# A neighbourhood-attention stage that scores only the keys it needs

## The chip, the cores and the metric

The kernel runs on one core of one Trainium2 chip. The metric is the time of the device in microseconds (us); smaller is better. A core has TensorE (PE in the profile, with PEld for its weight loads), VectorE (DVE), ScalarE (ACT), GpSimd (POOL) and SyncE (SP), which work through queues of their own and wait for one another by semaphores. Transfers are issued by SP and ACT and carried by 16 DMA engines.

## The reference

One encoder block on 1024 tokens of 1024 features: RMS norm, one input projection, a convolution group and an attention group side by side, an output projection with a residual, then a SwiGLU feed-forward layer with a residual. The part that matters here is the attention. The tokens form a grid of 16 rows and 64 columns. Each query attends to a window of 8 rows and 16 columns that is clamped inside the grid, with a learned bias for the offset:

```python
col_start = jnp.clip(cols - kw // 2, 0, GRID_W - kw)      # kw = 16, GRID_W = 64
def row_block(r):
    row_start = jnp.clip(r - kh // 2, 0, rows - kh)       # kh = 8, rows = 16
    ...
    s = jnp.einsum("bqhd,brqchd->bhqrc", q_r, k_win) * scale
    s = s + bias
    p = jax.nn.softmax(s, axis=(-2, -1))
    return jnp.einsum("bhqrc,brqchd->bqhd", p, v_win)
```

There are 8 heads of 64 features. Everything is float32.

## The kernel before

The order of all instructions is written out by hand; each engine takes its own in that order. First come the projections for keys, for the convolution, for queries and for values, with the taps of the convolution on VectorE beside them. In the same time the tables of the bias are made in DRAM (`bias_tables`): `t1` is filled with a large negative number and gets the runs of `rpb`, `tf` is filled likewise and gets windows of `t1`. These small transfers are strung between the weight loads on SP's queue, six for each step (`behind`).

**Tiles of the attention.** The queries are cut into 8 tiles of 128: two halves of the grid's rows (`rh` 0 and 1, 8 rows each) by four blocks of 16 columns (`cb`). A tile `s_` takes its half and block from `order`, which goes through `cb` 0, 3, 1, 2 and both halves of each. A tile's scores are taken against a rectangle of keys, `AR` rows by `ncol` columns from column `c0` on (`WIN`). A step `i` is one tile and one pair of heads (`hp`); there are 32.

**One step.** `score_mm` (L680) multiplies the queries by the rectangle of keys into PSUM, 288 or 384 columns for each of the two heads. `score_max` (L693, VectorE) adds the table of the bias, which is the large negative number outside a query's window, and takes the maximum; `score_exp` (L698, ScalarE) the exponential and the sum; `score_norm` (L709, GpSimd) the scaling by the sum. `flip` (L720, TensorE) transposes the weights in three groups of four rows of keys, and `flip_out` copies them back to SBUF (L727 on VectorE, L729 on ScalarE). `weigh` (L739, TensorE) multiplies them by the values, group by group, and sums in PSUM. From step 4 on one round of the loop holds the scores of steps i and i + 1, the transposes of i - 3 and i - 2, and the weighing of i - 5 and i - 4. The next round's scores take the PSUM that the copy of L727 frees.

**Values.** `value_out` (L447) stores the values of each 128 tokens to `vd` in DRAM on ACT's queue. `load_vw` (L660) fetches from there, on SP's queue, one row of the grid at a time, the `ncol` tokens of a window: `ncol` rows of 512 numbers (2 KB), for one or two groups at once. `vw[cb, g]` is the group of grid rows 4g to 4g + 3 of window `cb`. `load_window` fetches all four groups. The tables are fetched by `table` (L647), also on SP's queue. The order on that queue around the stage is: tables of the first three tiles, values of window 0, values of window 3, tables, and from step 8 on the last table and windows 1 and 2, then weights of the output projection (`wo00`, `wo02`).

Of the kernel before, what the change touches and what calls it, by code (L numbers as in the profile page):

```python
# [6 lines left out]
F32 = mybir.dt.float32  # L7
# [5 lines left out]
P = 128  # L13
# [4 lines left out]
NH = 8  # L18
HD = 64
# [3 lines left out]
EPS = 1e-6  # L23
NEG = -1e30
GW = 64
AR = 12
SIDE = (16, 17, 18, 19, 20, 21, 22)
WIN = ((0, 24, 8), (8, 32, 0), (24, 32, 0), (40, 24, 0))


def layout(v):
# [33 lines left out]
def body(tc, a):  # L65
    from contextlib import ExitStack
    with ExitStack() as ctx:
        build(ctx, tc, a)


def build(ctx, tc, a):
    nc = tc.nc
    pe, act, dve, pool = nc.tensor, nc.scalar, nc.vector, nc.gpsimd
# [3 lines left out]
    dr = ctx.enter_context(tc.tile_pool(name="dr", bufs=1, space=bass.MemoryType.DRAM))  # L77

    def T(tag, shape, bufs, name, dt=F32):
        return sb.tile(shape, dt, tag=tag, bufs=bufs, name=name)  # L80

    def G(name, dt=F32):
        return T("G", [P, 1024], 21, name, dt)
# [4 lines left out]
    def H(name, dt=F32):  # L88
        return T("H", [P, 4096], 7, name, dt)
# [4 lines left out]
    def SM(name, n=8):  # L94
        return T("sm", [P, 8], 12, name)[:, :n]

    def mm(name):
        return ps.tile([P, 512], F32, tag="mm", bufs=4, name=name)

    def tp(name):  # L100
        return ps.tile([P, 512], F32, tag="tp", bufs=2, name=name)

    def cv(name):
        return ps.tile([P, 1024], F32, tag="cv", bufs=1, name=name)
# [14 lines left out]
    def lr(w):  # L119
        return w[:, :512], w[:, 512:]  # L120
# [127 lines left out]
    ident = T("ident", [P, P], 1, "ident")  # L248
# [24 lines left out]
    for _ in range(9):  # L273
# [1 line left out]
    pool.affine_select(ident, ones, pattern=[[-1, P]], compare_op=OP.is_equal, fill=0.0,  # L275
                       base=0, channel_multiplier=1)
    qgs = T("qgs", [P, 1], 1, "qgs")
    t1 = [dr.tile([NH, 16, 15, ncol], F32, name=f"t1{ty}") for ty, ncol in enumerate((24, 32, 24))]
    tf = {(rh, ty): dr.tile([16, 8, NH, AR * t1[ty].shape[-1]], F32, name=f"tf{rh}{ty}")
          for rh in range(2) for ty in range(3)}  # L280

    def rstd_of(ss, scale, name):
# [159 lines left out]
    vd = dr.tile([S, 512], F32, name="vd")  # L442
# [61 lines left out]
    def bias_tables():  # L504
        neg = G("neg")
        pool.memset(neg, NEG)

        def fill1(ty):
            n = 15 * t1[ty].shape[-1]
            nc.sync.dma_start(t1[ty].rearrange("h j u b -> (h j) (u b)"), neg[:, :n])  # L510

        def fill2(rh, ty):
            n = 3 * AR * t1[ty].shape[-1] if ty != 1 else 2 * AR * 32
            for o in range(0, NH * AR * t1[ty].shape[-1], n):
                w = min(n, NH * AR * t1[ty].shape[-1] - o)
                nc.sync.dma_start(tf[rh, ty].rearrange("j i h c -> (j i) (h c)")[:, o:o + w], neg[:, :w])

        def run(ty, j):
            b0, shift = ((max(j - 8, 0), 15), (j, 7), (min(j, 8), 7))[ty]
            o = b0 - j + shift  # L520
            nc.sync.dma_start(t1[ty][:, j, :, b0:b0 + 16], a["rpb"][:, :, o:o + 16])

        def rows_of(rh, ty, i):
            ncol = t1[ty].shape[-1]
            a0 = max(i - 4, 0) if rh == 0 else min(i, 4)
            u0 = a0 - i + (7 if rh == 0 else 3)
            nc.sync.dma_start(tf[rh, ty][:, i, :, a0 * ncol:(a0 + 8) * ncol],
                              t1[ty][:, :, u0:u0 + 8, :].rearrange("h j u b -> j h (u b)"))
        for ty in (0, 2, 1):
            fill1(ty)  # L530
        for ty in (0, 2, 1):
            aside_dma.extend(lambda ty=ty, j=j: run(ty, j) for j in range(16))
            for rh in range(2):
                aside_dma.append(lambda rh=rh, ty=ty: fill2(rh, ty))
        for ty in (0, 2, 1):
            for rh in range(2):
                aside_dma.extend(lambda rh=rh, ty=ty, i=i: rows_of(rh, ty, i) for i in range(8))
# [30 lines left out]
    for kp in range(4):  # L568
        parts = []
# [66 lines left out]


    def table(rh, ty):
        n = AR * t1[ty].shape[-1]
        src = tf[rh, ty].rearrange("j i h c -> (j i) (h c)")  # L640
        if rh == 0 and ty == 0:
            parts = [(G(f"tab{k}")[:, :n * min(3, NH - 3 * k)], 3 * k) for k in range(3)]
        else:
            parts = [(H(f"tab{rh}{ty}")[:, :NH * n], 0)]
        heads = []
        for w, h0 in parts:
            nc.sync.dma_start(w, src[:, h0 * n:h0 * n + w.shape[-1]])  # L647
            heads += [w[:, o:o + n] for o in range(0, w.shape[-1], n)]
        return heads


    vwt, vw = {}, {}

    def load_vw(cb, *gs):
        c0, ncol, _ = WIN[cb]
        if gs[0] % 2 == 0:
            vwt[cb, gs[0] // 2] = G(f"vw{cb}{gs[0]}").rearrange("p (g d) -> p g d", d=512)
        w = vwt[cb, gs[0] // 2]
        for r in range(4):
            nc.sync.dma_start(w[r * ncol:(r + 1) * ncol, gs[0] % 2:gs[-1] % 2 + 1, :],  # L660
                              vd.rearrange("(g r c) d -> r c g d", r=4, c=GW)[r, c0:c0 + ncol, gs[0]:gs[-1] + 1, :])
        for g in gs:
            vw[cb, g] = w[:4 * ncol, g % 2, :]


    k4 = kT.rearrange("p c (r w) -> p c r w", w=GW)
    order = [(rh, cb) for cb in (0, 3, 1, 2) for rh in range(2)]
    tab, et, es, pTs, os_, sums, pp, mx, cvs = {}, {}, {}, {}, {}, {}, {}, {}, {}
    at = []

    def score_mm(i):
        s_, hp = divmod(i, 4)
        rh, cb = order[s_]
        t = rh * 4 + cb
        c0, ncol, _ = WIN[cb]
        s2 = cv(f"s{i}") if i > 0 and i % 2 == 0 else None
        out = []
        for hh in range(2):
            s = (mm(f"s{i}{hh}") if s2 is None else lr(s2)[hh])[:, :AR * ncol]
            pe.matmul(s, qT[hh * HD:(hh + 1) * HD, hp, t * P:(t + 1) * P],  # L680
                      k4[hh * HD:(hh + 1) * HD, hp, rh * 4:rh * 4 + AR, c0:c0 + ncol], start=True, stop=True)
            out.append(s)
        return out

    def score_max(i, hh, s):
        s_, hp = divmod(i, 4)
        rh, cb = order[s_]
        if i not in es:
            et[i] = G(f"e{i}").rearrange("p (h n) -> p h n", h=2)
            es[i] = et[i][:, :, :AR * WIN[cb][1]]  # L690
            sums[i] = SM(f"rs{i}", 2)
        mx[i, hh] = SM(f"mx{i}{hh}", 1)
        dve.tensor_tensor_reduce(out=es[i][:, hh], in0=s[hh], in1=tab[rh, cb][2 * hp + hh], scale=-1.0,  # L693
                                 scalar=3.0e38, op0=OP.add, op1=OP.min, accum_out=mx[i, hh])
# [15 lines left out]


    def flip(i):
        s_, hp = divmod(i, 4)
        m = 4 * WIN[order[s_][1]][1]
        if i % 2 == 0:
            cvs[i] = cv(f"p{i}")
        pp[i] = lr(cvs[i]) if i % 2 == 0 else [mm(f"p{i}{hh}") for hh in range(2)]
        for hh, pt in enumerate(pp[i]):
            for g in range(3):
                pe.transpose(pt[:m, g * P:(g + 1) * P], es[i][:, hh, g * m:(g + 1) * m], ident)  # L720

    def flip_out(i, hh=None):
        m = 4 * WIN[order[i // 4][1]][1]
        w = et[i][:m, :, :384]
        pTs[i] = [w[:, h].rearrange("p (n q) -> p n q", q=P) for h in range(2)]
        if hh is None:
            dve.tensor_copy(w, cvs[i].rearrange("p (h n) -> p h n", h=2)[:m, :, :384])  # L727
        else:
            act.copy(w[:, hh], pp[i][hh][:m, :384])  # L729

    def weigh(i):
        s_, hp = divmod(i, 4)
        rh, cb = order[s_]
        if hp == 0:
            os_[s_] = tp(f"o{s_}").rearrange("p (c q) -> p c q", c=4)
        for g in range(3):
            for hh in range(2):
                c = (2 * hp + hh) * HD
                pe.matmul(os_[s_][hh * HD:(hh + 1) * HD, hp], vw[cb, rh + g][:, c:c + HD], pTs[i][hh][:, g],  # L739
                          start=g == 0, stop=g == 2)  # L740

    def half(name):
        w = H(name, F32R).rearrange("p (w k s) -> p w k s", w=2, s=512)
# [15 lines left out]
    def value(t):  # L759
        z = nat(2, t, mm if t < 6 else tp)  # L760
        step(lambda n_taps: (value_out(t, z), pump(n_taps)))
# [3 lines left out]
    def load_window(cb):  # L765
        load_vw(cb, 0, 1)
        load_vw(cb, 2, 3)
# [12 lines left out]
    both(0, s0)  # L780
    pump(200)
    value(6)
    load_vw(0, 0, 1)
    load_vw(0, 2)
    s1, s3 = score_mm(1), score_mm(3)
    step()
    score_norm(0)
# [92 lines left out]
    for i in range(4, 32, 2):  # L880
# [24 lines left out]
        if i > 4:  # L905
            weigh(i - 5)
# [541 lines left out]
    def quarter(w, o, t):  # L1448
        return w[:, o + t * 512:o + t * 512 + 512]
# [32 lines left out]
    for s, p in enumerate(SEQ):  # L1482
        for k in range(QF - 2):
            n = s * QF + k
# [23 lines left out]
    for half in range(2):  # L1508
# [4 lines left out]
        w = quarter(om["u"], 0, 3)[:, part_]  # L1513
# [17 lines left out]
```

## Time and profile before

| what | value |
|---|---|
| median of 3 runs | 1035.13 us (1034.98 to 1036.01) |
| the profiled execution | 1035.18 us, its span 1033.5 us |
| TensorE busy | 1024.3 us (99%) |
| VectorE, ScalarE, GpSimd busy | 782.3 us (76%), 478.7 us (46%), 436.0 us (42%) |
| transfers | 152.53 MB in 75084 packets, 42.5% of the 16 engines' span on SP's queue (q1), 0.9% on ACT's (q10) |
| attention stage | about 220 to 306 us after the span's start |

The profile is of one execution. Times in it are counted from the first instruction; the 1.7 us between the span and the profiled execution lie outside. A line like `L739 PE MATMUL o<-e,vw` names the line of the kernel, the engine, the operation and the tiles written and read. A busy TensorE is not one at its peak, since matmuls overlap. The chain that ended last is followed back from the last instruction: at each step to what released it.

### The profile page before, as it was taken

Reading aid. Unit: us, or ns where it says so; the run is one execution under the profiler, and the core shown is the slowest. Engines: PE = TensorE matmul, PEld = TensorE weight load, DVE = VectorE, ACT = ScalarE, POOL = GpSimd, SP = SyncE. Lnnn points to the kernel's source line nnn. Section 1 sums busy time; section 2 is a strip of 40 time slices with the busy share of each in tenths; the row PEclk is TensorE's granted clock in tenths of the full one; section 3 lists DMA queues with packets and bytes.
Section 4 is the critical chain, followed back from the end, with each engine's and each line's share of the span. In section 5 each row is a group of like instructions: output and inputs, shape, how many; then the busy total and the mean of one; then the engine's idle time right before and its main releaser. Section 6 shows DMA issues by size and latency. Waiting matters only on the chain.

```text
span 1033.5 us, 15158 instructions
## 1 busy us (share of the span) xinstructions
PE 1024.3 (99%) x5334; PEld 853.8 (83%) x5334; DVE 782.3 (76%) x1234; ACT 478.7 (46%) x1045; POOL 436.0 (42%) x345
## 2 busy tenths in 40 slices
PE   9999999999999999999999999999999999999998
PEld 7888888877787788877888888888888888888887
DVE  5788997896755376998787787787787767758874
ACT  7565348836866345523334334343342443433432
POOL 1036764524641345047776667567566200003210
PEclk9999999999999999999999999999999999999999
DMA  9426781337403621122434424434441696633631
GB/s 347 165 79 201 225 255 53 122 115 234 124 22 122 235 92 41 47 107 89 156 119 157 139 96 153 153 101 145 144 143 71 222 365 238 224 102 123 214 122 42
DMA packets 75084, 152.53 MB, mean 148 GB/s; under 512 B 13824, under 2 KB 22784, under 8 KB 74368
## 3 DMA queue, kind: packets, MB, share of 16 engines
q1 hardware_dynamic: 72992, 148.21, 42.5%
q10 hardware_dynamic: 2016, 3.36, 0.9%
q8 instruction: 42, 0.69, 0.3%
q14 instruction: 34, 0.28, 0.1%
HBM read 112.38 MB, written 44.76 MB: 152 GB/s over the span
## 4 chain that ended last, share of the span: by engine, by line
PE 93%; DVE 5%; ACT 1%; issue 1%; DMA 0%; ACTq 0%; DVEq 0%
PE B L115 5%; PE B L116 5%; PE B L117 5%; PE z L115 4%; PE z L117 4%; PE z L116 4%; PE D L115 3%; PE D L116 3%; PE D L117 3%; PE gl L117 3%; PE gl L116 3%; PE gl L115 3%; PE pj L115 3%; PE pj L116 3%; PE pj L117 3%; PE p L720 2%
## 5 line engine op out<-in xcount | busy, mean ns | idle before, releaser
L363 DVE SCALAR_TENSOR_TENSOR cv<-u,par,cv 128x1009 f32<-128x1009 f32 (+14 forms) x92 | 117.4, 1277 | 2.3
L389 POOL TENSOR_TENSOR pa<-pa,pr 128x1022 f32<-128x1022 f32 (+5 forms) x24 | 58.0, 2417 | 48.7 <-ACT pr L388 36.1
L107 ACT CAST op<-sr 128x512 fp32r<-128x512 f32 x77 | 47.7, 619 | 57.7 <-PE B2d L117 26.7
L1474 POOL TENSOR_TENSOR ou<-ou,resm 128x512 f32<-128x512 f32 x8 | 12.0, 1506 | 139.8 <-DVE ou L1465 126.1
L111 DVE TENSOR_TENSOR op<-sr,op 128x512 fp32r<-128x512 f32 x77 | 57.6, 748 | 16.5 <-ACT op L107 16.4
L709 POOL TENSOR_SCALAR e<-e,rs 128x288 f32<-128x288 f32 (+1 forms) x64 | 33.9, 545 | 41.8 <-DVE rs L707 40.1
L1024 DVE TENSOR_TENSOR ts<-gu,ts 128x512 f32<-128x512 f32 x40 | 46.3, 1158 | 0.7
L107 ACT CAST op<-wd 128x512 fp32r<-128x512 f32 x54 | 33.4, 619 | 28.5 <-DVE wd L1370 18.0
L698 ACT ACTIVATE e<-e,mx 128x288 f32<-128x288 f32 (+1 forms) x64 | 36.5, 572 | 18.8 <-DVE mx L693 16.9
L111 DVE TENSOR_TENSOR op<-wd,op 128x512 fp32r<-128x512 f32 x54 | 39.8, 738 | 1.7 <-ACT op L107 0.6
L693 DVE CUSTOM_DVE_ANT_0 e<-s,tab 128x288 f32<-128x288 f32 (+1 forms) x64 | 28.7, 503 | 13.6 <-PE s L680 13.6
L980 POOL TENSOR_TENSOR sq<-sq,sq 128x512 f32<-128x512 f32 x12 | 17.1, 1423 | 51.6 <-ACT sq L976 51.4
L1283 DVE TENSOR_TENSOR g<-D,g 128x512 f32<-128x512 f32 x22 | 15.2, 690 | 23.4 <-PE D L117 23.4
L416 ACT ACTIVATE sq<-z,r 128x64 f32<-128x64 f32 x96 | 28.3, 329 | 5.2 <-PE z L117 5.2
L1260 ACT ACTIVATE D<-D 128x512 f32<-128x512 f32 x22 | 12.8, 582 | 32.6 <-DVE D L1259 32.6
L388 ACT ACTIVATE pr<-u,par 128x1022 f32<-128x1022 f32 (+5 forms) x24 | 27.0, 1138 | 1.6 <-ACT vs L446 1.2
L720 PEld LDWEIGHTS p<-ident,e 128*96 128x96 f32 (+1 forms) x192 | 20.5, 133 | 6.8 <-POOL e L709 6.3
L115 PE MATMUL B2d<-op 128*128 128x512 f32 x66 | 25.8, 391 | 0.0
L117 PE MATMUL B2d<-op 128*128 128x512 f32 x66 | 25.7, 389 | 0.0
L116 PE MATMUL B2d<-op 128*128 128x512 f32 x66 | 25.7, 389 | 0.0
L739 PE MATMUL o<-e,vw 96*64 96x128 f32 (+1 forms) x384 | 24.7, 277 | 0.0
L720 PE MATMUL p<-ident,e 128*96 128x128 f32 (+1 forms) x192 | 24.4, 276 | 0.0
(1454 smaller groups left out, 3734.5 us busy)
## 6 DMA issues: line engine op xcount, KB each, us to landing
gu<-in_gu SPq DMA_DIRECT2D x44, 512.0 KB
sr<-sd SPq DMA_DIRECT2D x77, 256.0 KB
sd<-sd SPq DMA_DIRECT2D x22, 512.0 KB
wd<-in_wd SPq DMA_DIRECT2D x36, 256.0 KB
sd<-g SPq DMA_DIRECT2D x33, 256.0 KB
x<-in_x SPq DMA_DIRECT2D x8, 512.0 KB
xT<-in_xp SPq DMA_DIRECT2D x8, 512.0 KB
xd<-xT SPq DMA_DIRECT2D x16, 256.0 KB
```

The source lines that it names most:

```text
L107: act.copy(hi, src)
L111: eng.tensor_tensor(*[w[..., sl] for w in (lo, src, hi.bitcast(F32))], OP.subtract)
L115: pe.matmul(acc, lh, rh, start=start, stop=False, skip_group_check=True)
L116: pe.matmul(acc, lh, rl, start=False, stop=False, skip_group_check=True)
L117: pe.matmul(acc, ll, rh, start=False, stop=stop, skip_group_check=True)
L363: dve.scalar_tensor_tensor(acc[:, o], uc[:, i], dwk[:, c, t:t + 1], acc[:, o], OP.mult, OP.add)
L389: pool.tensor_tensor(pa[:, o], pa[:, o], pr[:, o], OP.add)
L693: dve.tensor_tensor_reduce(out=es[i][:, hh], in0=s[hh], in1=tab[rh, cb][2 * hp + hh], scale=-1.0, scalar=3.0e38, op0=OP.add, op1=OP.min, a ...
L698: act.activation(e, e, AF.Exp, bias=mx.pop((i, hh)), scale=-1.0, accum_out=sums[i][:, hh:hh + 1])
L709: pool.tensor_scalar(es[i][:, hh], es[i][:, hh], rs[:, hh:hh + 1], 1.0, op0=OP.mult, op1=OP.mult)
L720: pe.transpose(pt[:m, g * P:(g + 1) * P], es[i][:, hh, g * m:(g + 1) * m], ident)
L1024: dve.tensor_tensor(o, l, r, OP.subtract)
```

## The change

The rectangle of keys shrinks to what the reference allows: 11 rows for the upper half of the grid and 12 for the lower, and 23, 31, 31 and 24 columns for the four blocks (before: 12 rows, 24, 32, 32 and 24 columns). The scores, the tables of the bias, the exponential and the scaling get narrower with it. The values of windows 0, 1 and 2 are loaded 23, 31 and 31 rows at a time. The keys of the first tile (11 x 23 = 253) form two groups of 128 instead of three (four rows of keys each), so its values come in a layout of their own (`load_first`: twelve loads, the sixth row of the grid cut at the group's edge into 13 and 10), and the loads of groups 1, 2 and 3 of window 0, for the second tile, follow. Where the last group is not full (tiles with 11 rows), GpSimd writes zeros behind the scores before the transposes. The table of the first tile comes in two parts of four heads instead of three of three.

```diff
-AR = 12
-WIN = ((0, 24, 8), (8, 32, 0), (24, 32, 0), (40, 24, 0))
+AR = (11, 12)
+WIN = ((0, 23), (8, 31), (24, 31), (40, 24))
+NCOL = (23, 31, 24)
...
 def load_vw(cb, *gs):
-    c0, ncol, _ = WIN[cb]
-    if gs[0] % 2 == 0:
+    c0, ncol = WIN[cb]
+    if (cb, gs[0] // 2) not in vwt:
         vwt[cb, gs[0] // 2] = G(f"vw{cb}{gs[0]}").rearrange("p (g d) -> p g d", d=512)
...
+def load_first():
+    c0, ncol = WIN[0]
+    w = vwt["first"] = G("vwf").rearrange("p (g d) -> p g d", d=512)
+    for r in range(AR[0]):
+        for g in range(2):
+            a0, a1 = max(r * ncol, g * P), min((r + 1) * ncol, g * P + P)
+            if a0 < a1:
+                t = r * GW + c0 + a0 - r * ncol
+                nc.sync.dma_start(w[a0 - g * P:a1 - g * P, g, :], vd[t:t + a1 - a0, :])
...
+def width(s_):
+    rh, cb = order[s_]
+    return AR[rh] * WIN[cb][1]
+
+def groups(s_):
+    n, m = width(s_), P if s_ == 0 else 4 * WIN[order[s_][1]][1]
+    return [slice(o, min(o + m, n)) for o in range(0, n, m)]
...
 def score_max(i, hh, s):
...
+        n, gs = width(s_), groups(s_)
+        es[i] = et[i][:, :, :n]
+        if n < len(gs) * gs[0].stop:
+            pool.memset(et[i][:, :, n:len(gs) * gs[0].stop], 0.0)
...
 def flip(i):
...
-            for g in range(3):
-                pe.transpose(pt[:m, g * P:(g + 1) * P], es[i][:, hh, g * m:(g + 1) * m], ident)
+            for g, k in enumerate(gs):
+                pe.transpose(pt[:m, g * P:(g + 1) * P], et[i][:, hh, k.start:k.start + m], ident)
...
 def weigh(i):
...
-    for g in range(3):
+    gs = groups(s_)
+    for g, k in enumerate(gs):
+        n = k.stop - k.start
+        v = vwt["first"][:, g, :] if s_ == 0 else vw[cb, rh + g]
...
-    load_vw(0, 0, 1)
+    load_first()
+    load_vw(0, 1)
     load_vw(0, 2)
```

More of the change, by code (lines that the diff above doesn't have):

```diff
@@ L277, in build @@
     qgs = T("qgs", [P, 1], 1, "qgs")
-    t1 = [dr.tile([NH, 16, 15, ncol], F32, name=f"t1{ty}") for ty, ncol in enumerate((24, 32, 24))]
-    tf = {(rh, ty): dr.tile([16, 8, NH, AR * t1[ty].shape[-1]], F32, name=f"tf{rh}{ty}")
+    t1 = [dr.tile([NH, 16, 15, ncol], F32, name=f"t1{ty}") for ty, ncol in enumerate(NCOL)]
+    tf = {(rh, ty): dr.tile([16, 8, NH, AR[rh] * NCOL[ty]], F32, name=f"tf{rh}{ty}")
           for rh in range(2) for ty in range(3)}
@@ L508, in fill1 @@
         def fill1(ty):
-            n = 15 * t1[ty].shape[-1]
+            n = 15 * NCOL[ty]
             nc.sync.dma_start(t1[ty].rearrange("h j u b -> (h j) (u b)"), neg[:, :n])
         def fill2(rh, ty):
-            n = 3 * AR * t1[ty].shape[-1] if ty != 1 else 2 * AR * 32
-            for o in range(0, NH * AR * t1[ty].shape[-1], n):
-                w = min(n, NH * AR * t1[ty].shape[-1] - o)
+            n = (3 if ty != 1 else 2) * AR[rh] * NCOL[ty]
+            for o in range(0, NH * AR[rh] * NCOL[ty], n):
+                w = min(n, NH * AR[rh] * NCOL[ty] - o)
                 nc.sync.dma_start(tf[rh, ty].rearrange("j i h c -> (j i) (h c)")[:, o:o + w], neg[:, :w])
@@ L523, in rows_of @@
         def rows_of(rh, ty, i):
-            ncol = t1[ty].shape[-1]
+            ncol = NCOL[ty]
             a0 = max(i - 4, 0) if rh == 0 else min(i, 4)
@@ L638, in table @@
     def table(rh, ty):
-        n = AR * t1[ty].shape[-1]
+        n = AR[rh] * NCOL[ty]
         src = tf[rh, ty].rearrange("j i h c -> (j i) (h c)")
         if rh == 0 and ty == 0:
-            parts = [(G(f"tab{k}")[:, :n * min(3, NH - 3 * k)], 3 * k) for k in range(3)]
+            parts = [(G(f"tab{k}")[:, :4 * n], 4 * k) for k in range(2)]
         else:
@@ L674, in score_mm @@
         t = rh * 4 + cb
-        c0, ncol, _ = WIN[cb]
+        c0, ncol = WIN[cb]
         s2 = cv(f"s{i}") if i > 0 and i % 2 == 0 else None
@@ L678, in score_mm @@
         for hh in range(2):
-            s = (mm(f"s{i}{hh}") if s2 is None else lr(s2)[hh])[:, :AR * ncol]
+            s = (mm(f"s{i}{hh}") if s2 is None else lr(s2)[hh])[:, :width(s_)]
             pe.matmul(s, qT[hh * HD:(hh + 1) * HD, hp, t * P:(t + 1) * P],
-                      k4[hh * HD:(hh + 1) * HD, hp, rh * 4:rh * 4 + AR, c0:c0 + ncol], start=True, stop=True)
+                      k4[hh * HD:(hh + 1) * HD, hp, rh * 4:rh * 4 + AR[rh], c0:c0 + ncol], start=True, stop=True)
             out.append(s)
@@ L689, in score_max @@
             et[i] = G(f"e{i}").rearrange("p (h n) -> p h n", h=2)
-            es[i] = et[i][:, :, :AR * WIN[cb][1]]
+            n, gs = width(s_), groups(s_)
+            es[i] = et[i][:, :, :n]
+            if n < len(gs) * gs[0].stop:
+                pool.memset(et[i][:, :, n:len(gs) * gs[0].stop], 0.0)
             sums[i] = SM(f"rs{i}", 2)
@@ L712, in flip @@
     def flip(i):
-        s_, hp = divmod(i, 4)
-        m = 4 * WIN[order[s_][1]][1]
         if i % 2 == 0:
@@ L718, in flip @@
         for hh, pt in enumerate(pp[i]):
-            for g in range(3):
-                pe.transpose(pt[:m, g * P:(g + 1) * P], es[i][:, hh, g * m:(g + 1) * m], ident)
+            gs = groups(i // 4)
+            m = gs[0].stop
+            for g, k in enumerate(gs):
+                pe.transpose(pt[:m, g * P:(g + 1) * P], et[i][:, hh, k.start:k.start + m], ident)
     def flip_out(i, hh=None):
-        m = 4 * WIN[order[i // 4][1]][1]
-        w = et[i][:m, :, :384]
+        gs = groups(i // 4)
+        m, n = gs[0].stop, len(gs) * P
+        w = et[i][:m, :, :n]
         pTs[i] = [w[:, h].rearrange("p (n q) -> p n q", q=P) for h in range(2)]
         if hh is None:
-            dve.tensor_copy(w, cvs[i].rearrange("p (h n) -> p h n", h=2)[:m, :, :384])
+            dve.tensor_copy(w, cvs[i].rearrange("p (h n) -> p h n", h=2)[:m, :, :n])
         else:
-            act.copy(w[:, hh], pp[i][hh][:m, :384])
+            act.copy(w[:, hh], pp[i][hh][:m, :n])
     def weigh(i):
@@ L735, in weigh @@
             os_[s_] = tp(f"o{s_}").rearrange("p (c q) -> p c q", c=4)
-        for g in range(3):
+        gs = groups(s_)
+        for g, k in enumerate(gs):
+            n = k.stop - k.start
+            v = vwt["first"][:, g, :] if s_ == 0 else vw[cb, rh + g]
             for hh in range(2):
                 c = (2 * hp + hh) * HD
-                pe.matmul(os_[s_][hh * HD:(hh + 1) * HD, hp], vw[cb, rh + g][:, c:c + HD], pTs[i][hh][:, g],
-                          start=g == 0, stop=g == 2)
+                pe.matmul(os_[s_][hh * HD:(hh + 1) * HD, hp], v[:n, c:c + HD], pTs[i][hh][:n, g],
+                          start=g == 0, stop=g == len(gs) - 1)
     def half(name):
```

## The prediction

> **What bounds the kernel now.** I read the page first (busy shares and the chain that ended last), then the windows of the attention stage, then the chain in that stage, then what the transfers there do.
>
> ```profile
> span 1033.5 us, 15158 instructions
> PE 1024.3 (99%) x5334; PEld 853.8 (83%) x5334; DVE 782.3 (76%) x1234; ACT 478.7 (46%) x1045; POOL 436.0 (42%) x345
> ...
> PE 93%; DVE 5%; ACT 1%; issue 1%; DMA 0%; ACTq 0%; DVEq 0%
> ```
>
> TensorE is busy for 99% of the span and carries 93% of the chain. No transfer is on the chain. The attention stage, the only one that the change touches heavily, looks the same:
>
> ```profile
> core 0: us, PE busy (x) PEld busy (x) DVE busy (x) ACT busy (x) POOL busy (x), PEclk, DMA share, GB/s
> 220.00:306.00 86.00, 85.69 (x795) 65.89 (x794) 59.44 (x192) 59.81 (x182) 39.62 (x72) 1.00 0.39 123
> ```
>
> Its chain, in order of time, is a repetition of scores (s), transposes (p) and weighing by the values (o), one round for two head pairs:
>
> ```profile
> 238.44 0.97 DVE e L727
> ...
> 246.21 1.46 PE o L739 x24
> ...
> 251.75 1.17 PE s L680 x8
> 252.92 1.45 PE p L720 x12
> 254.37 1.46 PE o L739 x24
> ...
> 271.65 1.46 PE o L739 x24
> ...
> 286.35 1.49 PE s L680 x8
> 287.84 1.46 PE p L720 x12
> 289.30 1.46 PE o L739 x24
> ```
>
> The rounds follow without a gap, so here a column or a matmul less on TensorE shortens the kernel, as long as what TensorE waits for comes no later. Between the 24-column tiles (251.75) and the 32-column tiles (286.35) only the scores grow, by 0.32 us for 96 columns.
>
> **Scores.** One round is two head pairs, so a column costs 0.32/96/2 = 1.67 ns per head pair. Per head pair the change takes off 35, 12, 24, 0, 43, 12, 43 and 12 columns in the eight tiles, four head pairs each: 181 x 4 x 1.67 ns = 1.2 us.
>
> **Two groups in the first tile.** Eight transposes go (1.45/12 = 0.12 us each) and sixteen matmuls of o (1.46/24 = 0.061 us each): 1.0 + 1.0 us. But the weighing is also what covers VectorE's copy of the transposes before the next scores can take the same PSUM:
>
> ```profile
> L727 DVE COPY e<-p x16: 953/955/958, 233.7 to 297.5; 96x768 f32<-96x768 f32 x8, 128x768 f32<-128x768 f32 x8
> ```
>
> The copy was already exposed once (238.44 in the chain). With 16 instead of 24 matmuls (0.97 us) it comes out by 0.1 to 0.2 us in one more round; I take back 0.3 us in all. Sum on TensorE: 3.2 - 0.3 = 2.9 us less, if nothing else comes late.
>
> **VectorE, ScalarE.** Their score rows get shorter with TensorE's, and both wait for TensorE in this stage; nothing on the path.
>
> **The memsets on GpSimd.** Sixteen are new, of 6, 48 or 62 elements per partition. Two rows bound one of them, and a third shows the idle time in front of the instructions that they now precede:
>
> ```profile
> L270 POOL MEMSET ones<- x1: 205/205/205, 0.8 to 0.8; 128x128 f32 x1
> ...
> L506 POOL MEMSET neg<- x1: 957/957/957, 59.9 to 59.9; 128x1024 f32 x1
> ...
> POOL e L709 <- DVE rs L707: 40.1, 20, 14.2
> ```
>
> At most 0.2 us each, 3.3 us together, in 40 us of waiting for VectorE: nothing. Queued behind each is the scaling (L709) of two head pairs, for which the transposes wait; without that cover a round would lose up to 0.4 us, 8 rounds 3.3 us.
>
> **The bias tables.** The same number of transfers carries 3 to 12% fewer bytes, from addresses that are no longer round. The weight loads share the queue; the closest is w03l, ready at 140.1 + 2.85 = 142.95 and used at 144.7. So up to 1.7 us of delay is free; I take nothing and leave 2 us in the range.
>
> ```profile
> L116 PEld LDWEIGHTS z<-w03l,hT x16: 187/188/188, 144.7 to 185.8; 128*128 128x128 f32 x16
> ...
> L111 POOL TENSOR_TENSOR w03l<-w03r,w03h x1: 2850/2850/2850, 140.1 to 140.1; 128x1024 fp32r<-128x1024 f32 x1
> ```
>
> **The value loads: the term that decides.** These fetch 24 or 32 rows of 2 KB from vd; now it is 23 or 31 (the window at column 40 keeps 24). Two windows of the transfers, the first from 217.5 to 222.5, the second from 229.5 to 235, show how one is spread over the 16 DMA engines:
>
> ```profile
> q1 hardware_dynamic: 192, 0.30, 19.3%
> ...
> vw<-vd SPq DMA_DIRECT2D x2, 96.0 KB
> vw<-vd SPq DMA_DIRECT2D x2, 48.0 KB
> ```
>
> ```profile
> q1 hardware_dynamic: 144, 0.20, 12.8%
> q10 hardware_dynamic: 144, 0.26, 12.8%
> ...
> vw<-vd SPq DMA_DIRECT2D x4, 48.0 KB
> ```
>
> In the second, q10 carries one store of 128 rows: 128 packets, and 16 more. q1 carries four loads of 24 rows: 96 packets, and 48 more, 12 for each load. In the first, four loads with 144 rows again have 48 more. The extra packets are the completions, one from each engine used. So 128 rows use 16 engines with eight rows each, and 24 rows use 12 with two each, though 16 were there: every engine used gets the same number of rows, by the count of rows and not of packets (24 x 2 also takes 12). 23 and 31 are prime: equal shares then mean one engine. That is my reading; the other, two rows to an engine with the last one short (12 and 16 engines), is a rival, for no row has a prime count.
>
> The Trainium skill has the rule (DMA: Bandwidth & Descriptors, Why a DMA increments its semaphore by 16 and not by 1): a load from SP uses the largest number up to 16 that divides the rows on both sides, always the lowest-numbered engines, and 127 partitions use one. By that rule the forecast is this case; the trace agrees for 24 and 128 rows and shows nothing for a prime.
>
> If all land on one and the same engine, they queue there, in order. What a 2 KB packet costs, from a full window and from the loads of xT between 315 and 320:
>
> ```profile
> 248.00:250.00 2.00, 2.00 (x19) 1.57 (x16) 1.59 (x9) 1.32 (x5) 0.48 (x2) 1.00 1.06 450
> ...
> q1 hardware_dynamic: 546, 1.55, 86.3%
> ...
> xT<-in_xp SPq DMA_DIRECT2D x4, 512.0 KB
> ```
>
> 450 GB/s over 16 engines at a share of 1.06 is 26.5 GB/s each, 77 ns for 2 KB; the xT loads took 0.863 x 16 x 5.0 us for 1.55 MB, 91 ns for 2 KB. The short value loads above took 0.128 x 16 x 5.5 us for 96 rows, 117 ns with their start-ups. In a long queue there are few start-ups; I take 84 ns, the middle of the first two, and keep 77 and 117 as ends.
>
> The order on SP's queue, with the times at which its parts can begin:
>
> ```profile
> 209.71 0.32 SPq L647 DMA_DIRECT2D tab<-tf  x1
> ...
> 227.66 0.33 ACTq L447 DMA_DIRECT2D vd<-vs  x1
> ...
> 229.68 0.29 SPq L660 DMA_DIRECT2D vw<-vd  x1
> ...
> 263.25 0.42 SPq L660 DMA_DIRECT2D vw<-vd  x1
> ```
>
> The first engine's share of the table issued at 209.71 is 8 rows of 8.4 KB, 2.6 us at 26.5 GB/s: free at 212.6. Then come, through that one engine: for the first tile 10 x 23 rows, and one each of the loads of 13 and 10 rows, which spread; for the second tile 4 x 23 and 8 x 23: 508 packets, 42.7 us. ScalarE's stores of four value tiles add 4 x 8 packets, 2.7 us. They stand at 258.0. A store is seen 229.68 - 227.66 = 2.0 us after its issue; less the issue (0.33) and its own packets (0.7), landing takes 1.0 us: 259.0. The second tile's weighing wants them in the round at 246.21, in its second half, 246.9: TensorE waits 12 us, though 1.6 us of the saving came before. Then 32 packets of the 24-row loads (2.7 us) and three tables (8 rows each of 9.2, 10.9 and 11.9 KB, 9.7 us): 270.4. The window at column 8 is eight loads of 31 x 2 = 62 packets, 41.7 us: 312.0, landed 313.0, wanted at 271.65 + 0.73 = 272.4. The window at column 24 is the same again: 353.7, landed 354.7, wanted at 289.30 + 0.73 = 290.0. The engine never runs dry (SP issues in 0.4 us what takes 2 to 5 us), so the last need sets the delay: 354.7 - 290.0 = 64.7 us. The 2.9 us saved on TensorE lie ahead of that wait and are swallowed. Queued behind these loads on SP are wo00 and wo02 (after 263.25), which were used only after 300 and still have time.
>
> After a long wait TensorE may restart slowly, as at the start of the program:
>
> ```profile
> L274 PEld LDWEIGHTS up<-ones x18: 192/333/334, 1.0 to 4.4; 128*128 128x128 f32 x18
> ```
>
> 3.4 us at 333 instead of 192 ns lose 1.4 us, once, for earlier restarts are swallowed too. The Trainium skill (TensorE: Matmul & The Clock Gate, Part 1) has the clock halved after an idle window of about 3.4 us; an estimate from that page for one restart is 1.7 us. The page of this profile shows a clock of 9 in every slice, so no row tests it within the stage.
>
> The profiled execution took 1035.18 us, its span 1033.5, the median of the runs is 1035.13. Sum: 1035.2 + 64.7 + 1.4 = **1101.3 us**.
>
> **Rivals.** First, *the loads stay spread* (two rows to an engine). Every load then lands within 2 us of its issue, as now, and the saving stands: 1035.2 - 2.9 = 1032.3 us, faster by 0.28%. For it: 24 rows on 12 engines fit it as well. Against it: no engine here had a short share. It decides from the point where a packet's share of the queue falls below (290.0 - 1.0 - 212.6 - 15.1)/1500 = 41 ns, 15.1 us being the tables, the stores and the 24-row loads. Second, *one engine for each load, but a different one each time*: 62 packets then take 5.2 us, side by side, and the second tile's loads, issued by 240, land by 246; 1032.3 to 1034 us. For it: no row tells which engine was used. Against it: the equal spread needs no rotation. Third, within my reading, *the packets' price*: 77 ns gives 212.6 + 1500 x 0.077 + 14.6 + 1.0 = 343.7, a delay of 53.7 and 1090 us; 117 ns gives 212.6 + 175.5 + 17.2 + 1.0 = 406.3, 116.3 us and 1153 us, with start-ups on every packet, which a long queue will not have.
>
> **How the numbers follow.** 0.85 for one engine: equal shares are all that the trace has, and the case needs only that they hold for a prime. 0.09 and 0.06 for the two others. A measurement of this kernel tells about 0.2% (2 us) from no change. The first two rivals mostly clear it, short of the bias tables' and the memsets' risks: faster 0.11, same 0.03, slower 0.86. The range holds the one-engine case from 69 ns a packet (1078; a tenth under the full window, should one engine alone run quicker) to 109 ns (1140; start-ups on three packets of four); the 2 us of the bias tables are inside it, the first two rivals outside.
>
> **What would show it.** Right: a window of the transfers between 270 and 310 with a DMA share near 1/16 (0.06) and about 24 GB/s; the same 992 packets over some 83 us; the groups of o (L739's successor) waiting for vw loads in the tiles two, five and seven of the order, about 12, 29 and 24 us; TensorE's busy share falling to about 93%. Scores at 1.67 ns per column and head pair and eight transposes fewer would still hold. Wrong: vw loads with 12 or more completions each, a stage that ends about 3 us earlier, or waits in another place, such as transposes waiting for GpSimd.

## The result and the profile after

The changed kernel takes 1098.2 us (median of five runs, 1097.76 to 1098.91); the kernel before took 1035.37 us beside it (1034.98 to 1036.13). The ratio is 1.0606, 95% interval 1.059 to 1.0621: slower by 62.8 us. The forecast was 1101.3 us, with a range of 1078 to 1140.

The page of the changed kernel's profiled execution (1098.2 us), its first lines, the granted clock, SP's queue and the shares of the chain that ended last:

```profile
span 1096.5 us, 15139 instructions
...
PE 1033.6 (94%) x5310; PEld 858.8 (78%) x5310; DVE 779.9 (71%) x1234; ACT 477.5 (44%) x1045; POOL 436.5 (40%) x361
...
PEclk9999999997875999999999999999999999999999
...
q1 hardware_dynamic: 72622, 147.26, 39.6%
...
PE 81%; DMA 7%; DVE 7%; SPq 3%; ACT 1%; issue 1%; ACTq 0%; DVEq 0%
```

Transfers, absent from the chain before, now carry 7% of it, and SP's issuing 3%. TensorE has 24 instructions fewer but 9 us more of busy time: the clock row shows four slices (27 us each, from 247 to 356 us) under 9. What TensorE waited for between 205 and 380 us (us in total, times, longest; shorter waits left out):

```profile
PE o L765 <- DMA vw<-vd: 49.3, 5, 15.3
PE p L742 <- ACT e L752: 5.0, 1, 5.0
```

The chain in the stage, in order of time. First its beginning:

```profile
227.75 5.33 DMA vd<-vs
...
234.36 8.42 DMA vw<-vd
...
242.80 0.02 ACTq L448
...
242.86 5.40 DMA vd<-vs
...
248.53 13.08 DMA vw<-vd
...
261.74 0.71 PE o L765 x4
```

And then the two later waits, with a warm round between them:

```profile
289.13 20.71 DMA vw<-vd
309.93 0.70 PE o L765 x4
310.63 2.78 PE s L699 x8
...
318.54 1.46 PE p L742 x12
...
321.47 1.35 PE s L699 x8
...
330.00 21.90 DMA vw<-vd
351.99 0.70 PE o L765 x4
352.68 2.78 PE s L699 x8
355.46 1.78 PE p L742 x12
```

The weighing (o, L765, was L739) stands still until the values are there at 261.7, 309.9 and 352.0: tiles two, five and seven. In the first 3 us after a wait a group of scores (s) takes 2.78 instead of 1.35 us. What the transfers do between 275 and 305 us:

```profile
DMA packets 373, 0.77 MB, mean 26 GB/s; under 512 B 6, under 2 KB 6, under 8 KB 372
...
q1 hardware_dynamic: 372, 0.75, 6.6%
...
vw<-vd SPq DMA_DIRECT2D x7, 124.0 KB
```

A share of 6.6% is one sixteenth of 16 engines: one works all the time, 15 do nothing. In 30 us some six loads of 62 packets end and leave six completions (the packets under 512 B), one for each.

### The profile page after: what moved, and what is told of

It is laid out like the page before. It is cut to its first block, busy times and chain, and to the rows that moved or that the text cites. A ratio compares the mean times of both kernels' runs of the same rounds, so it can differ in the third digit from the quotient of the medians.

```text
span 1096.5 us, 15139 instructions
## 1 busy us (share of the span) xinstructions
PE 1033.6 (94%) x5310; PEld 858.8 (78%) x5310; DVE 779.9 (71%) x1234; ACT 477.5 (44%) x1045; POOL 436.5 (40%) x361
## 4 chain that ended last, share of the span: by engine, by line
PE 81%; DMA 7%; DVE 7%; SPq 3%; ACT 1%; issue 1%; ACTq 0%; DVEq 0%
DMA vw<-vd 6%; PE B L116 5%; PE B L117 5%; PE B L118 5%; PE D L116 3%; PE D L117 3%; PE D L118 3%; PE z L116 3%; PE z L118 3%; PE z L117 3%; SPq L661 3%; PE gl L116 3%; PE gl L118 3%; PE gl L117 3%; PE pj L116 3%; PE pj L117 2%
## 5 line engine op out<-in xcount | busy, mean ns | idle before, releaser
L715 DVE CUSTOM_DVE_ANT_0 e<-s,tab 128x341 f32<-128x341 f32 (+5 forms) x64 | 27.5, 481 | 68.1 <-PE s L699 68.0
L731 POOL TENSOR_SCALAR e<-e,rs 128x341 f32<-128x341 f32 (+5 forms) x64 | 33.1, 531 | 104.9 <-DVE rs L729 78.9
L720 ACT ACTIVATE e<-e,mx 128x341 f32<-128x341 f32 (+5 forms) x64 | 35.3, 553 | 82.6 <-DVE mx L715 72.6
L765 PE MATMUL o<-e,vw 124*64 124x128 f32 (+2 forms) x336 | 24.7, 291 | 49.3 <-DMA vw<-vd 49.3
L765 PEld LDWEIGHTS o<-e,vw 124*64 124x64 f32 (+2 forms) x336 | 19.2, 143 | 53.3 <-issue 53.1
L742 PEld LDWEIGHTS p<-ident,e 128*124 128x124 f32 (+3 forms) x184 | 22.6, 149 | 13.5 <-issue 9.4
L742 PE MATMUL p<-ident,e 128*124 128x128 f32 (+3 forms) x184 | 27.5, 303 | 5.1 <-ACT e L752 5.0
L699 PE MATMUL s<-kT,qT 64*128 64x341 f32 (+5 forms) x128 | 25.7, 523 | 0.3 <-DVE e L750 0.3
L116 PE MATMUL B2d<-op 128*128 128x512 f32 x66 | 25.8, 391 | 0.0
```

The source lines that it names most:

```text
L116: pe.matmul(acc, lh, rh, start=start, stop=False, skip_group_check=True)
L720: act.activation(e, e, AF.Exp, bias=mx.pop((i, hh)), scale=-1.0, accum_out=sums[i][:, hh:hh + 1])
L731: pool.tensor_scalar(es[i][:, hh], es[i][:, hh], rs[:, hh:hh + 1], 1.0, op0=OP.mult, op1=OP.mult)
L742: pe.transpose(pt[:m, g * P:(g + 1) * P], et[i][:, hh, k.start:k.start + m], ident)
L765: pe.matmul(os_[s_][hh * HD:(hh + 1) * HD, hp], v[:n, c:c + HD], pTs[i][hh][:n, g], start=g == 0, stop=g == len(gs) - 1)
```

## The experiments

The theory: a load uses as many engines as divide its rows equally, so one for 23 or 31 rows, and the engine's queue is the whole loss. The rivals: other parts of the change (tables, memsets, the first tile) share the guilt; or odd loads are slow whatever engines they use.

**1. The change, with loads that divide.** Each load of 23 or 31 rows is cut into 16 and the rest.

```diff
         for r in range(4):
-            nc.sync.dma_start(w[r * ncol:(r + 1) * ncol, ...], ...[r, c0:c0 + ncol, ...])
+            for b0, b1 in (((0, 16), (16, ncol)) if ncol % 2 else ((0, ncol),)):
+                nc.sync.dma_start(w[r * ncol + b0:r * ncol + b1, ...], ...[r, c0 + b0:c0 + b1, ...])
```
(and likewise in `load_first`)

> The change, with each load of 23 or 31 rows cut into 16 rows and the rest (7 or 15); the same bytes, about twice as many loads. Theory (a load uses the largest number of engines that divides its rows, a prime uses one): 16, 15 and 7 engines, no long queue, the waits for vw are gone, and the saving on TensorE that I predicted remains: 1035.2 - 2.9 = 1032.3 us. Rival (the other parts of the change, the unround tables or the memsets, cost something that the waits covered): over 1034 us, up to 1036. Rival (loads from unround rows are slow however many engines they use): waits for vw remain, over 1045 us.

Measured: 1032.84 us against 1035.50 of the kernel before beside it, ratio 0.9975 (0.9966 to 0.9984). The waits are gone; the transfers between 258 and 270 us:

```profile
DMA packets 1058, 1.46 MB, mean 121 GB/s; under 512 B 355, under 2 KB 355, under 8 KB 1057
...
vw<-vd SPq DMA_DIRECT2D x12, 60.0 KB
vw<-vd SPq DMA_DIRECT2D x11, 64.0 KB
```

Twelve loads of 15 rows and eleven of 16 would leave 12 x 15 + 11 x 16 = 356 completions if each row count is the count of its engines; 355 are there. The same bytes in twice as many loads: the rows' divisors decide, and nothing else of the change costs what the waits could have covered. This version beats both kernels, and holds what I had expected of the change without its waits (1032.3).

**2. The kernel before, with prime loads only.** 24 rows are cut into 23 + 1 in window 0, 32 into 31 + 1 in windows 1 and 2.

```diff
-            nc.sync.dma_start(w[r * ncol:(r + 1) * ncol, ...], ...[r, c0:c0 + ncol, ...])
+            for b0, b1 in (((0, ncol - 1), (ncol - 1, ncol)) if cb < 3 else ((0, ncol),)):
+                nc.sync.dma_start(w[r * ncol + b0:r * ncol + b1, ...], ...[r, c0 + b0:c0 + b1, ...])
```

> The kernel before, with each load of 24 rows of window 0 cut into 23 + 1 and each load of 32 rows of windows 1 and 2 into 31 + 1; nothing else of the change. Theory (23, 31 and 1 row each use the same one engine; 82 ns for a packet, as the last wait of the changed kernel gives: (352.0 - 1.0 - 212.6 - 15.1)/1500): windows 1 and 2 are 1024 packets, 84.2 us from their first issue at 259.6: 344.8, wanted at 290.0, so 54.8 us and 1.4 for the restart: 1091 us. Rival (the two groups, memsets or tables share the guilt): well under that, 1036 to 1070.

Measured: 1097.91 us in one run. No other part of the change is in it, and it loses as much as the whole change (1098.2). That the two times agree to 0.3 us is partly chance: here the tables are through at 265.4 us, in the change at about 273, and the last need then waits for 16 loads of 64 packets, in the change for 15 loads of 62 (see below). That it is 7 us above the 1091 is an error of mine in this sum: I let the windows start with their first issue, but the tables go ahead of them on the queue. Between 262 and 270 us the full rate, mostly 246 to 614 GB/s, lasts until 265.4 (17 slices of 0.2 us):

```profile
GB/s 553 430 246 553 369 553 246 614 369 492 369 307 553 369 553 307 184 0 82 82 92 31 92 20 31 20 31 20 31 20 31 31 31 20 31 20 31 20 31 20
```

265.4 + 84.2 + 1.0 = 350.6; in its chain the last wait ends at 351.3.

**3. The kernel before, with prime loads in the last window only.**

```diff
+            for b0, b1 in (((0, ncol - 1), (ncol - 1, ncol)) if cb == 2 else ((0, ncol),)):
```

> The kernel before, with only the loads of the last window (column 24) cut into 31 + 1. Theory (a queue at one engine, in order, so that only its length counts): 512 packets from 261.9 on at 82 ns are over at 304.0, landed at 305.0, wanted at 290.0: 15 us, and 1.4 for the restart: 1051.6 us. Rival (each odd load costs a fixed wait wherever it stands, a third of the 62.8 us for each of the three windows): 1056 us. Rival (it takes all the windows together for the delay, as the loads are hidden else): 1035 us.

Measured: 1052.43 us in one run. The wait and the chain behind it:

```profile
PE o L740 <- DMA vw<-vd: 14.5, 1, 14.5
```

```profile
290.36 15.06 DMA vw<-vd
...
306.25 2.86 PE s L681 x8
309.11 1.76 PE p L721 x12
```

One wait of 14.5 us, ended at 305.4 (expected 305.0). A queue's length counts, not the number of odd loads: each of the three windows does not cost a third.

**4. Four grid rows in one load.** 92 or 124 rows of 2 KB in a load; the first tile's loads of 23 rows stay.

```diff
+        if ncol % 2:
+            for g in gs:
+                nc.sync.dma_start(w[:4 * ncol, g % 2, :],
+                                  vd.rearrange("(g r c) d -> g r c d", r=4, c=GW)[g, :, c0:c0 + ncol, :])
```

> The change, with the four grid rows of a group of a 23- or 31-column window in one load (92 or 124 rows of 2 KB); the first tile's loads of 23 stay. Theory (largest divisor up to 16): 92 and 124 rows use 4 engines with 23 or 31 rows each, so 4 completions for each load; a window is 124 packets on each of four engines, 10.2 us from about 258: landed near 270, just in time: 1032.3 to 1034 us. Rival (equal shares rounded up, 8 rows to an engine with one short): 16 completions for each load (12 for 92 rows), 1032.3 us. Rival (one engine as soon as the last part is prime): 1098 us again.

Measured: 1036.63 us in one run, 2.6 us above the expected end. The transfers between 262 and 270 us, then the chain at the start of the stage:

```profile
DMA packets 402, 0.81 MB, mean 102 GB/s; under 512 B 12, under 2 KB 12, under 8 KB 401
...
q1 hardware_dynamic: 401, 0.80, 26.2%
```

```profile
236.78 5.46 DMA vd<-vs
...
242.29 5.98 DMA vw<-vd
...
250.38 2.52 PE p L746 x12
```

Four engines as expected: a share of a quarter, 102 GB/s, and 389 packets of 2 KB in 8 us are about three loads of 124, with four completions each. The window at column 8 no longer made anything wait. What I had missed is the first tile, whose loads still sit on one engine: the last store of the values stands behind them for 5.46 us, the second tile's last group comes late (1.8 us of waiting), and the following transposes take 2.52 instead of 1.45 us.

**5. Four grid rows in one load, and the first tile's 23 rows as 16 + 7.** This tests that reading.

```diff
+                    for b0, b1 in (((a0, a0 + 16), (a0 + 16, a1)) if a1 - a0 == ncol else ((a0, a1),)):
```

> As the version with a group's four grid rows in one load (4 engines), and the first tile's loads of 23 rows cut into 16 + 7. Theory (what that version lost, 3.8 us, came from the first tile's loads at one engine, behind which the last store of the values took 5.5 us): 1032.8 us, the store about 2 us. Rival (four engines are too few by themselves): 1036 again.

Measured: 1032.87 us, ratio 0.9975 (0.9965 to 0.9984). The issue of the last store, and that of the load which fetches what it stores:

```profile
236.29 0.33 ACTq L448 DMA_DIRECT2D vd<-vs  x1
...
238.35 0.60 SPq L662 DMA_DIRECT2D vw<-vd  x1
```

The store was done within 2.06 us. Four engines are enough; the 3.8 us came from the first tile's one engine.

**6. The odd column apart.** 22 or 30 rows, and the last columns of a group's grid rows in one load.

```diff
+        k = ncol // 2 * 2
+        for r in range(4):
+            nc.sync.dma_start(d4[r * ncol:r * ncol + k], s4[r, :k])
+        if k < ncol:
+            nc.sync.dma_start(d4[k:4 * ncol:ncol], s4[:, k])
```

> The change, with the loads of 23 and 31 rows shortened to 22 and 30, and the last column of a group's grid rows (4 or 5 rows of 2 KB, one grid row apart) in a load of its own; 10 loads for a window in place of 16 in the version with 16 and the rest. Theory (largest divisor up to 16): 11, 15, 4 and 5 engines, no queue, 1032.8 us as with 16 and the rest. Rival (the number of loads on SP counts): faster than that by 0.4 us for each round that waited for an issue, at most 1032.0. Rival (rows a grid row apart are slow): over 1034.

Measured: 1032.81 us, ratio 0.9974 (0.9965 to 0.9984). Ten loads for a window do as well as sixteen: the issues on SP are hidden in both.

**7. Three groups in the first tile.** As experiment 1, with the first tile's groups of four grid rows kept.

```diff
-        n, m = width(s_), P if s_ == 0 else 4 * WIN[order[s_][1]][1]
+        n, m = width(s_), 4 * WIN[order[s_][1]][1]
```

> As the version with 16 and the rest, but the first tile keeps three groups of four grid rows (92, 92 and 69 keys), so that only the narrower scores, tables and softmax of the change are left. Theory (my sum): the scores are worth 1.2 us: 1035.4 - 1.2 = 1034.2 us, and the two groups the other 1.5 of the 2.7 us that were measured. Rival (the exposed copy eats what the two groups save): 1032.8. Rival (the scores are worth nothing): 1035.4.

Measured: 1033.89 us, ratio 0.9982 (0.9973 to 0.9991) to 1035.57: the scores' part is 1.7 us, 0.9 to 2.8 by the interval, so 1.2 fits; the two groups are left with about 1.1 (1033.89 - 1032.84), uncertain by as much, since each ratio is known to about 0.9 us either way. The chain tells why less than my 1.7. A round of the first tile with three groups, from one group of scores to the next, and the same round with two groups (experiment 1):

```profile
239.73 1.20 PE s L701 x8
...
243.84 1.09 PE s L701 x8
```

```profile
239.04 1.20 PE s L701 x8
...
241.72 0.97 DVE e L752
...
242.73 1.16 PE s L701 x8
```

4.11 us become 3.69, a gain of 0.42, where two transposes and eight matmuls (0.24 + 0.49) were saved: with the weighing shorter, VectorE's copy stands in the chain.

**8. The memsets five times.** As experiment 1.

```diff
-                pool.memset(et[i][:, :, n:len(gs) * gs[0].stop], 0.0)
+                for _ in range(5):
+                    pool.memset(et[i][:, :, n:len(gs) * gs[0].stop], 0.0)
```

> As the version with 16 and the rest, but each memset is done five times (80 instead of 16, 0.14 us each: 9.2 us more on GpSimd). Theory (they run while GpSimd waits for VectorE): 1032.8 us, within 0.3. Rival (they stand ahead of the scaling that the transposes wait for): 16 steps x 4 x 0.14 = up to 9 us more, 1042; half of that if every second one is hidden.

Measured: 1032.89 us, ratio 0.9973 (0.9963 to 0.9984). The group of the memsets (ns: least, median, most):

```profile
L715 POOL MEMSET e<- x80: 102/144/159, 215.3 to 284.1; 128x62 f32 x40, 128x6 f32 x20, 128x48 f32 x20
```

64 x 0.144 = 9.2 us more on GpSimd change nothing.

## Why the prediction was right, step by step

**One engine for a prime count: right.** It was read from 24 rows on 12 engines and 128 on 16, and the chance of 0.85 rested on that alone. The completions show it in four new cases (31: one, 15: 15, 16: 16, 124: four), and experiment 2 shows that it is enough for a loss of this size. This is the rule of the Trainium skill (DMA: Bandwidth & Descriptors, Why a DMA increments its semaphore by 16 and not by 1), the largest number up to 16 that divides the rows; the runs agree in each of these counts. The two rivals with spread loads fall with the waits that are there; that one engine is the same for all loads is seen in the share, which stays at one sixteenth throughout a stretch in which six loads end.

**The packet's price: right.** From the landing of one window to that of the next, 309.9 to 352.0, are 42.1 us for eight loads, 496 packets: 85 ns, where I took 84.

**Landing times: 261.7, 309.9 and 352.0 against 259.0, 313.0 and 354.7.** The first is later by 2.7, the others sooner by 3. That is what two slips of mine left, which partly cancel.

Later, since the queue on the engine began later than I had it. I had the engine free of the first table at 212.6. The rate of all engines between 212 and 222 us stays full for 12 slices of 0.25 us, until 215:

```profile
GB/s 237 304 439 270 473 372 338 439 372 249 410 328 123 41 25 33 41 41 57 25 82 205 410 336 172 41 82 33 16 25 25 25 25 25 25 33 25 25 25 25
```

So up to 2.4 us come from the start. I had also counted four stores beside the loads, but five were issued from 210 us on (210.79, 216.23, 227.75, 228.89 and 242.86). The stores themselves now took 5.33 and 5.40 us instead of 2 (see below) and SP's loads waited for them, but that did not leave the engine idle: between 232 and 242 us, part of such a wait, 120 packets of 2 KB went through it, 83 ns each.

Sooner, since I let tile five wait for all eight loads of its window, and it waits for seven. TensorE in that tile, with what ended its idle time before (in brackets):

```profile
294.65 1.12 PE L765 MATMUL o<-e,vw 124*64 124x128 f32 x8 [5.50 <-DMA vw<-vd]
309.93 0.70 PE L765 MATMUL o<-e,vw 93*64 93x128 f32 x4 [14.16 <-DMA vw<-vd]
```

With 11 grid rows in the rectangle the last group holds three of them, 93 keys, and `weigh` reads only these (`v[:n]`); the load of the fourth row is not needed until tile six. Between 273 and 309 us:

```profile
DMA packets 458, 0.97 MB, mean 27 GB/s; under 512 B 21, under 2 KB 21, under 8 KB 451
```

451 - 21 = 430 packets of 2 KB are seven loads of 62 (434, to within the few at the ends), not eight (496). Nor had any of the window gone through beside the tables: its loads are issued from 263.35 on, and between 264 and 273 us no packet of 2 KB passes. All 33 packets under 8 KB are completions (under 512 B), and the tables, whose rows are longer, have the engines to themselves:

```profile
DMA packets 389, 3.83 MB, mean 426 GB/s; under 512 B 33, under 2 KB 33, under 8 KB 33
```

The same holds for tile seven, which also has 11 rows. The load too many is 62 x 0.084 = 5.2 us in the sum: 354.7 - 5.2 + 2.7 = 352.2, where 352.0 was measured. So the path was right, but the forecast came nearer to the time than its terms deserved. The 82 ns that I took into experiments 2 and 3 were worked out with the same two slips; that they fitted there (351.3 - 1.0 - 265.4 over 1024 packets are 83 ns) was partly luck.

**The last need sets the delay, and TensorE's saving is swallowed: right.** 352.0 - 290.0 = 62.0 us and 1.75 for the restart (below) come to 63.8, where the two profiled executions differ by 63.0; what makes the 0.8 between them stays open. Experiment 2 has none of the saving. Its last weighing goes on at 351.6, that of the change at 352.0, and from there both need 746 us to the end (1097.91 - 351.6, 1098.2 - 352.0): behind the wait nothing of the saving is left to see.

**The waits' places: right, their sizes near.** 8.2, 19.7 and 21.4 us in tiles two, five and seven, 49.3 in all, where I named 12, 29 and 24; TensorE's busy share is 94% (93 expected). The waits count only standing still, and TensorE was also slower after each of them, which counts as busy. And 5.0 us lay in a place that I had not named: the first tile's transposes, waiting for ScalarE.

**The restart: 1.4 us expected, 1.75 seen** after the last wait: scores 2.78 and transposes 1.78, where warm rounds have 1.35 and 1.46. In experiment 3 the granted clock after its wait:

```profile
core 0: us, PE busy (x) PEld busy (x) DVE busy (x) ACT busy (x) POOL busy (x), PEclk, DMA share, GB/s
305.50:309.00 3.50, 3.44 (x12) 1.51 (x12) 1.04 (x4) 0.46 (x1) 0.00 (x0) 0.50 0.06 25
309.00:311.00 2.00, 2.00 (x18) 1.79 (x18) 1.14 (x6) 1.86 (x8) 0.54 (x1) 0.82 0.04 13
311.00:313.00 2.00, 2.00 (x30) 1.83 (x27) 1.67 (x4) 1.98 (x5) 1.43 (x4) 1.00 0.00 0
```

Half the clock for 3.5 us and full from 311 on. By an estimate from the half clock and the 3.4 us of the Trainium skill (TensorE: Matmul & The Clock Gate, Part 1) such a restart costs 1.7 us; these rows agree with it better than my rows from the program's start did.

**Scores: right.** Warm rounds of experiment 1 in the tiles of 11 x 31 and 12 x 31 keys:

```profile
280.28 1.35 PE s L701 x8
284.55 1.45 PE s L701 x8
```

Before they took 1.49: 0.14 us for 43 columns are 1.6 ns per column and head pair. **Two groups:** expected 1.7 after the copy's 0.3, measured about 1.1, with an uncertainty as large as the difference. In the round that experiment 7 shows the copy takes back 0.3 us by itself (0.73 saved, 0.42 gained). **Memsets at nothing: right** (experiment 8). **Tables, VectorE, ScalarE at nothing:** experiment 1, which has them all, gains 2.7 us where 2.9 were expected, so together they cost nothing that its interval (1.7 to 3.5 us) shows.

## What to carry to other kernels

Look at the row count of each transfer as well as at its bytes: 23 or 31 rows sit on one engine at 25 GB/s, while 16 + 7, 22 and a column, or four rows of the grid in one load are all fast. When a transfer's shape changes, work out its engines' queue and compare each landing with the time at which it is wanted; the last late one sets the end. Count for each need which loads it really waits for: here one load of eight was 5.2 us. A change that trims work on the bounding engine can be right in that (here 2.7 us of 1035) and still lose 60 in a transfer that the profile before shows as hidden.

## What the runs showed of the hardware that I had not expected

A busy engine makes a well spread transfer late too. The store of 128 rows of values on ACT's queue, between 241 and 249 us of the changed kernel:

```profile
GB/s 20 31 20 20 31 20 31 20 20 31 20 31 20 215 358 420 328 31 31 20 31 20 20 31 20 31 20 31 102 31 20 31 20 20 31 20 31 20 31 61
...
q10 hardware_dynamic: 144, 0.26, 8.6%
```

Nearly all of its 256 KB go through in four slices of 0.2 us, but it counts as done only after 5.40 us, when its eight packets on the busy engine are through. Before, a store took 2.0 us. The engine is thus shared by both queues.

And ScalarE itself was held up: in the chain, the issue of that store (ACTq L448, 242.80) follows on a load of SP's queue (vw<-vd, to 242.78), and ScalarE's copies are queued behind that issue, so TensorE's transposes waited 5.0 us for them. Why the store waits for that load the profile doesn't say, and I didn't test it.
